# Four landing tiles for weights in a pool of their own, in layer 0 and layer 1's first half

## The chip, the core and the metric

The kernel runs on one core of one Trainium2 chip. The core's engines are TensorE (PE: matmuls, with a weight load, PEld, beside each), VectorE (DVE), ScalarE (ACT), GpSimd (POOL) and SyncE (SP), which issues all of this kernel's DMAs. The metric is the device time of one execution in microseconds.

## The reference

One inference step of a decoder trunk with two layers and width D = 1024, for a prompt of 1024 tokens and for 8 short sequences of 4 tokens (32 sample tokens), each with states of its own. Cut to what matters here:

```
def trunk(x):                       # rows of 1024 prompt tokens, or of 32 sample tokens
    h = x
    # layer 0 (even): S5 and HGRN2 side by side
    u, z_a, q, f, i, z_b = split(rmsnorm(h, norm_w[0]) @ even_w_in)     # 1024 x 3072
    y = gelu(s5(u))                                                     # complex diagonal state space
    a = y * sigmoid(y @ ssm_glu_w + glu_b) * silu(z_a)                  # 512 columns
    b = rms(hgrn2(silu(q), sigmoid(-f), i)) * silu(z_b)                 # 4 heads, 512 columns
    h = h + concat(a, b) @ even_w_out                                   # 1024 x 1024
    # layer 1 (odd): RWKV-7
    xn = rmsnorm(h, norm_w[1]);  xx = previous_row(xn) - xn
    xr, xw, xk, xv, xa, xg = (xn + xx * mix[m] for m in range(6))
    r, k, v, z = xr @ W[0], xk @ W[1], xv @ W[2], xg @ W[3]             # rw_w_rkvz, 1024 x 1024 each
    decay = exp(-c * sigmoid(w0 + tanh(xw @ w1) @ w2));  a = sigmoid(a0 + (xa @ a1) @ a2)
    g = sigmoid(xg @ g1) @ g2
    y, state = rwkv7_scan(r, decay, k, v, kk, a, state)                 # 16 heads of 64
    h = h + ((groupnorm(y) + bonus) * g * silu(z)) @ rw_w_o
    return rmsnorm(h, final_norm_w), all states
```

## The kernel before

Activations lie with the width on the partitions and the tokens along the free axis, in two halves: the first 512 tokens, and the other 512 with the 32 sample tokens (544 columns, as two cuts of 272). All matmuls are done in parts: each operand is split into a rounded high part and the rest, and each product of a weight tile (128x128) and an operand is the sum of three, high by high, high by low, low by high (`dense2`, line 805: `wh`,`xh`; `wh`,`xl`; `wl`,`xh`).

A weight is a column block of 128 out of a matrix, with eight tiles of 128 rows. `weights2` makes it: two DMAs of 256 KB each bring four row tiles into a **landing tile** `ws` (line 784); ACT copies it into the high part `wh` (line 70), DVE subtracts that from `ws` and writes the low part `wl` (line 72). `wh` and `wl` have two buffers each, so the next weight's are written when the matmuls with the last but one are done. The landing tile, too, has two buffers, in the pool `wp` with `wh` and `wl`. A landing tile comes free when `wl` has been made from it. `lora_weights` does the same for the low-rank weights `w1` and `a1` of RWKV-7, but for each half of the rows it takes two landing tiles: `ws`, which is loaded, and `wm`, into which POOL multiplies the same weights by `mix` (line 961).

The operands come as pairs, `xh` and `xl`, from `pair`: nine pairs in the pool `xx`, and in one stage `nxe` more, in the pool `xe` that exists only there (the second loop over `first` in `halves`: layer 1's first half, after the output projection of layer 0 has ended).

The program runs in stages. **Layer 0**: the input projection (`proj_in`) of half 1 and half 0 for the first four column blocks, then the other twenty blocks of each half, woven with S5 and the HGRN2 heads; `l1_vectors` loads small vectors of layer 1 (`mix`, by elements of 4 bytes) after the second block and makes `omix` from it on DVE (line 885). **Output of layer 0** (`glu`, `proj_out`): the S5 branch's gate, four weights, then eight weights of `even_w_out`, first for half 0 and then for half 1, this woven with the first steps of layer 1 (`l1_first`, which begins with `lora_weights`). Operands of the S5 branch and the heads are split by `cut` or `cut_in` (`gh`, `gl`). **Layer 1, first half**: k, r, v and the gate's first weights; then `layer1` runs the recurrence (chains over `ZR` and `BK`, which go through DRAM, line 1514) woven with the second half's projections, and the output projection.

The program's text gives the order only in part. A tile scheduler plays it through with estimated times and writes out for each engine one order, which the engine then follows; on SP this is the order of the DMA issues. Making a weight has high priority in it, so a DMA of a weight is put where a landing tile is estimated to be free. So another number of tiles changes the order on every engine.

Of the kernel before, what the change touches and what calls it, by code (L numbers as in the profile page):

```python
# [9 lines left out]
F32 = mybir.dt.float32  # L10
# [26 lines left out]
class Builder:  # L37
    def __init__(self, tc, I, O):
        self.tc, self.nc, self.I, self.O = tc, tc.nc, I, O
        self.load = {"act": 0.0, "dve": 0.0}  # L40
        self.tsz, self.inv = (200, 200, 160), [("v", 0, 32)]
        self.evb, self.ahead = 1.5, 4
        self.wcount, self.wpool, self.ev8 = 0, 0, [None, None]
        self.wp8 = dict(k=0, r=0, v=0), dict(k=1, r=1, v=1)
        self.pairs, self.nxe, self.per, self.xe = 0, 5, 2, None
        self.ly, self.lt = 4, (2, 4)
        self.lead = 2
        self.rate0, self.rate, self.rate2 = (1.4, 2.2, 1.0, 0.75), 1.5, 2.0
        self.nxh = 9
# [726 lines left out]
    def weights2(self, src, nk, m=128, name="w"):  # L776


        with self.tc.high_priority():
            wh = self.wp.tile([128, nk, m], F32R, tag="wh", name=f"{name}h", bufs=2)  # L780
            wl = self.wp.tile([128, nk, m], F32R, tag="wl", name=f"{name}l", bufs=2)
            for k in range(0, nk, 4):
                ke = min(k + 4, nk)
                ws = self.wp.tile([128, 4, m], F32, tag="ws", name=f"{name}s", bufs=2)
                if isinstance(src, list):
                    for h in range(2):
                        self.dma(ws[64 * h:64 * h + 64], src[k // 4].rearrange("p (k m) -> p k m", m=m))
                else:
                    self.dma(ws[:, :ke - k], src.rearrange("(k p) m -> p k m", p=128)[:, k:ke])
                self.wcount += 1  # L790
                self.split(wh[:, k:ke], wl[:, k:ke], ws[:, :ke - k], lo_pool=self.wcount % 8 < self.wpool)
        return wh, wl
# [157 lines left out]
    def lora_weights(self, names):  # L950

        with self.tc.high_priority():
            T = lambda tag: self.wp.tile([128, KT, 128], F32R, tag=tag, name=tag, bufs=2)
            plain, scaled = (T("wh"), T("wl")), (T("wh"), T("wl"))
            for k in range(0, KT, 4):
                ws, wm = (self.wp.tile([128, 4, 128], F32, tag="ws", name="ws", bufs=2) for i in range(2))
                for i, (nm, m) in enumerate(names):
                    cs = slice(64 * i, 64 * i + 64)
                    self.dma(ws[:, :, cs], self.I[f"rw_{nm}1"][0].rearrange("(k p) m -> p k m", p=128)[:, k:k + 4])
                    j = m * KT + k  # L960
                    self.nc.gpsimd.tensor_tensor(out=wm[:, :, cs], in0=ws[:, :, cs], op=ALU.mult,
                                                 in1=self.mix[:, j:j + 4].unsqueeze(2).broadcast_to([128, 4, 64]))
                for (h, l), x in ((plain, ws), (scaled, wm)):
                    self.split(h[:, k:k + 4], l[:, k:k + 4], x)
        return plain, scaled
# [860 lines left out]
    def build(self):  # L1826
        tc, nc, I = self.tc, self.nc, self.I
        dt = lambda name, shape: tc.dram_tile(shape, F32, name=name)
        self.xT_d = [dt(f"xT{k}", [128, NT]) for k in range(KT)]
        self.pr_d = {m: dt(f"pr{m}", [128, NT]) for m in range(4, 24)}  # L1830
        self.u_d = [dt(f"u{m}", [128, 8, 144]) for m in range(4)]
        self.y_d = [dt(f"y{m}", [128, 8, 136]) for m in range(4)]
        self.cat_d = [dt(f"cat{m}", [128, NT]) for m in range(4)]
        self.h1_d = [dt(f"h1{m}", [128, NT]) for m in range(KT)]

        H = lambda nm, sh: [[dt(f"{nm}{h}{g}", sh) for g in range(2)] for h in range(2)]
        self.zr_d, self.bk_d = H("zr", [128, 8, NP, 2, 64]), H("bk", [128, 8, NP, 2, 64])
        self.vc_d = H("vc", [128, 8, NP, 64])
        self.n_d, self.x_d, self.xn_d = H("nd", [128, 8, NP, 32]), H("xd", [128, 8, NP, 64]), H("xnd", [32, 2, 8, NP, 32])

        self.g1_d, self.g2_d = ([dt(f"{x}{h}", [128, 8, KT, 64]) for h in range(2)] for x in ("g1", "g2"))
        self.g1s_d, self.g2s_d, self.os_d = (dt(x, [128, KT, 32]) for x in ("g1s", "g2s", "os"))
        self.o_d = [dt(f"o{h}", [128, KT, 512]) for h in range(2)]
        self.pc_d = [dt(f"pc{m}", [2, NB, 64]) for m in range(KT)]
        for nm in ("r", "k", "v", "sw", "a"):
            setattr(self, f"{nm}_d", [dt(f"{nm}d{m}", [128, NT]) for m in range(KT)])
        self.rk_d = [dt(f"rkd{m}", [128, NT]) for m in range(KT)]
        with tc.tile_pool(name="cst", bufs=1) as self.cp:
            self.constants()
            self.nw0 = self.vec(I["norm_w"][0], "nw0")  # L1850
            with ExitStack() as st:
                self.pools(st)
                with ExitStack() as aux:
                    self.layer0(aux)
                with ExitStack() as aux:
                    self.halves(aux)

    def run(self, *gs, back=None):

# [68 lines left out]

            self.run((rest(), 1), (hgrn, self.rate0[2]))

    def halves(self, st):

        P = lambda name, st, **kw: st.enter_context(self.tc.tile_pool(name=name, bufs=1, reuse_waits="tile", **kw))
        R = lambda name, st: P(name, st, side="right")
        with ExitStack() as right:
            self.dp0, self.diff = R("diff", right), []
            with ExitStack() as r:
                op = R("out", r)
                with ExitStack() as t:
                    gp = P("glu1", t)  # L1940
                    glu = self.glu(1, gp, op)
                    next(glu)
                    self.heads_out(1, op)
                    next(glu)
                    self.norm1(0, lambda: gp.tile([128, 544], F32, tag="n", name="n", bufs=3))
                    for _ in glu:
                        pass
                rk = P("rwk", st)
                self.l1_pools(st)
                self.rwkv_constants(rk)  # L1950
                self.l1_constants(rk)
                self.made = {"v": [0, 0], "g": [0, 0], "x": 0, "o": [0, 0, 0], "first": False}
                self.ah, first = None, self.l1_first(0)
                self.run((self.proj_out(1), 1), back=(first, self.rate0[3]))
            self.ah, self.xe = R("ahead", right), R("xe", right)
            for _ in first:
                pass
            self.xe, gate = None, self.l1_gate(0)
            next(gate)
        self.ch = R("chn", st)  # L1960
        self.layer1(gate)

# [46 lines left out]
```

## Time and profile before

| what | us |
|---|---|
| median of 3 runs | 1949.92 |
| lowest and highest run | 1946.46, 1953.49 |
| profiled execution | 1946.68 |
| its span | 1945.0 |
| PE busy | 1736.1 (89%) |
| DVE busy | 1256.1 (65%) |
| ACT busy | 979.8 (50%) |
| POOL busy | 507.5 (26%) |

The mean granted clock of PE in the profiled execution is 0.903 of its full speed. The DMA queues moved 308.40 MB. The profile's views used below are the timeline of an engine (start, duration, instruction, and in brackets the idle time before it with what ended it), the waits of an engine summed by what it waited for, a tile's view (what its handlers waited for, and who waited for them), and windows (busy time of each engine in a stretch, granted clock, mean share of busy DMA engines, GB/s). A DMA share near 1 means that all 16 DMA engines are at work throughout.

### The profile page before, as it was taken

Reading aid. Unit: us, or ns where it says so; the run is one execution under the profiler, and the core shown is the slowest. Engines: PE = TensorE matmul, PEld = TensorE weight load, DVE = VectorE, ACT = ScalarE, POOL = GpSimd, SP = SyncE. Lnnn points to the kernel's source line nnn. Section 1 sums busy time; section 2 is a strip of 40 time slices with the busy share of each in tenths; the row PEclk is TensorE's granted clock in tenths of the full one; section 3 lists DMA queues with packets and bytes.
Section 4 is the critical chain, followed back from the end, with each engine's and each line's share of the span. In section 5 each row is a group of like instructions: output and inputs, shape, how many; then the busy total and the mean of one; then the engine's idle time right before and its main releaser. Section 6 shows DMA issues by size and latency. Waiting matters only on the chain. (4 is left out here: it accounts for less than half of the span.)

```text
span 1945.0 us, 39798 instructions
## 1 busy us (share of the span) xinstructions
PE 1736.1 (89%) x15060; PEld 1437.8 (74%) x15060; DVE 1256.1 (65%) x2700; ACT 979.8 (50%) x1887; POOL 507.5 (26%) x567
## 2 busy tenths in 40 slices
PE   6989889889979689998579999999899999999977
PEld 5767768788868577576447787888788888778776
DVE  5887778655554953689585852478979454655543
ACT  6345656354553434753345756565547434534464
POOL 2413535323221500001042410133322112331231
PEclk9989989887889899898779997999799899998799
DMA  9545444433544446699928424469795666544453
GB/s 242 150 128 153 112 116 134 121 112 107 154 148 152 128 150 199 199 243 263 247 66 219 140 88 129 130 168 276 191 235 160 164 160 166 151 130 128 121 151 112
DMA packets 555013, 308.40 MB, mean 159 GB/s; under 512 B 284884, under 2 KB 489044, under 8 KB 554821
## 3 DMA queue, kind: packets, MB, share of 16 engines
q1 hardware_dynamic: 554820, 305.86, 57.3%
q8 instruction: 119, 1.95, 0.4%
q14 instruction: 74, 0.60, 0.1%
HBM read 199.76 MB, written 104.81 MB: 157 GB/s over the span
## 5 line engine op out<-in xcount | busy, mean ns | idle before, releaser
L805 PE MATMUL dps<-xh,wh 128*128 128x272 f32 (+3 forms) x1696 | 589.5, 353 | 59.4 <-ACT wh L70 25.0
L805 PE MATMUL dps<-xl,wh 128*128 128x272 f32 (+3 forms) x1696 | 585.3, 347 | 7.8 <-DVE xl L72 6.1
L805 PE MATMUL dps<-xh,wl 128*128 128x272 f32 (+3 forms) x1696 | 581.9, 345 | 5.1 <-DVE wl L72 4.9
L805 PEld LDWEIGHTS dps<-xh,wh 128*128 128x128 f32 x1696 | 335.2, 200 | 110.6 <-ACT wh L70 29.9
L805 PEld LDWEIGHTS dps<-xh,wl 128*128 128x128 f32 x1696 | 338.6, 200 | 48.6 <-DVE wl L72 11.2
L805 PEld LDWEIGHTS dps<-xl,wh 128*128 128x128 f32 x1696 | 338.6, 200 | 47.7 <-DVE xl L72 8.2
L70 ACT ACTIVATE wh<-ws 128x512 fp32r<-128x512 f32 (+1 forms) x336 | 198.8, 620 | 331.8 <-PE dps L805 181.7
L72 DVE TENSOR_TENSOR wl<-ws,wh 128x512 fp32r<-128x512 f32 (+1 forms) x321 | 238.2, 756 | 139.3 <-ACT wh L70 125.5
L1514 PE MATMUL m<-ZR,BK 64*128 64x128 f32 x512 | 68.3, 311 | 10.4 <-DMA ZR<-zr 10.4
L1514 PEld LDWEIGHTS m<-ZR,BK 64*128 64x128 f32 x512 | 56.9, 206 | 19.6 <-DMA ZR<-zr 10.5
L70 ACT ACTIVATE xh<-mm 128x256 fp32r<-128x256 f32 (+1 forms) x112 | 52.9, 483 | 34.0 <-DVE mm L944 15.0
L805 PE MATMUL dps<-gh,wh 128*128 128x272 f32 (+1 forms) x176 | 56.3, 321 | 11.3 <-ACT wh L70 4.3
L72 POOL TENSOR_TENSOR xl<-mm,xh 128x256 fp32r<-128x256 f32 (+1 forms) x40 | 33.1, 828 | 111.6 <-ACT xh L70 89.0
L805 PE MATMUL dps<-gh,wl 128*128 128x272 f32 (+1 forms) x176 | 55.4, 316 | 7.3 <-DVE wl L72 7.3
L805 PE MATMUL dps<-gl,wh 128*128 128x272 f32 (+1 forms) x176 | 55.8, 317 | 5.6 <-DVE gl L72 5.6
L1411 DVE TENSOR_TENSOR sT<-sX,sN 128x31 f32<-128x31 f32 (+15 forms) x124 | 50.3, 405 | 5.2 <-DMA sN<-nd 2.8
L1417 DVE TENSOR_TENSOR sX<-sX,sT 128x31 f32<-128x31 f32 (+15 forms) x124 | 50.8, 410 | 2.3
L72 POOL TENSOR_TENSOR e<-ek,e 128x512 fp32r<-128x512 f32 (+1 forms) x16 | 22.0, 1376 | 114.5 <-ACT e L70 87.9
L72 DVE TENSOR_TENSOR xl<-mm,xh 128x512 fp32r<-128x512 f32 (+2 forms) x72 | 42.6, 599 | 12.7 <-PE t L1104 7.3
L64 ACT ACTIVATE ev<-dps 128x272 f32<-128x272 f32 (+1 forms) x65 | 29.4, 452 | 41.9 <-PE dps L805 36.4
L66 DVE COPY ev<-dps 128x272 f32<-128x272 f32 (+1 forms) x43 | 22.4, 523 | 42.9 <-PE dps L805 36.3
L805 PEld LDWEIGHTS dps<-gh,wh 128*128 128x128 f32 x176 | 36.0, 205 | 16.3 <-ACT ev L723 4.8
(651 smaller groups left out, 3676.4 us busy)
## 6 DMA issues: line engine op xcount, KB each, us to landing
ws<-in_rw_w_rkvz SPq DMA_DIRECT2D x128, 256.0 KB
ws<-in_even_w_in SPq DMA_DIRECT2D x96, 256.0 KB
ws<-in_rw_w_o SPq DMA_DIRECT2D x48, 256.0 KB
ws<-in_even_w_out SPq DMA_DIRECT2D x32, 256.0 KB
BK<-bk SPq DMA_DIRECT2D x32, 256.0 KB
ZR<-zr SPq DMA_DIRECT2D x32, 256.0 KB
pr<-ev SPq DMA_DIRECT2D x20, 272.0 KB
pr<-ev SPq DMA_DIRECT2D x20, 256.0 KB
```

Source lines behind the costliest of these rows:

```text
L64: return self.nc.scalar.activation(out, in_, AF.Copy)
L66: return self.nc.vector.tensor_copy(out, in_)
L70: self.nc.scalar.activation(hi, x, AF.Copy)
L72: e.tensor_tensor(out=lo, in0=x, in1=hi.bitcast(F32), op=ALU.subtract)
L805: mm = lambda c0, n, i, u, k, v: self.nc.tensor.matmul(ps[c0], u[:, k, :], v[:, c0:c0 + n], start=i == 0, stop=i == len(terms) - 1)
L1411: E.tensor_tensor(out=w, in0=X[:, s0:s0 + m, j:j + 1].broadcast_to([128, m, n]), in1=N[:, j, j + 1:32].unsqueeze(1).broadcast_to([128, m, ...
L1417: E.tensor_tensor(out=X[:, s0:s0 + m, j + 1:32], in0=X[:, s0:s0 + m, j + 1:32], in1=w, op=ALU.subtract)
L1514: nc.tensor.matmul(f2(pm[h][:, q]), f2(BK[hr, q]), f2(ZR[hr, q]), start=True, stop=True)
```

## The change

The landing tiles get a pool of their own, `ws`, on the right side of SBUF, with four buffers. It is opened ahead of layer 0 and closed after the gate's first weight in layer 1's first half; from there on a pool `ws1` with two buffers takes its place, as before. The number of additional operand pairs, `nxe`, goes from 5 to 4, so 13 pairs instead of 14 in the stage of layer 1's first half.

```diff
--- before.py
+++ after.py
@@ -42,7 +42,7 @@
         self.evb, self.ahead = 1.5, 4
         self.wcount, self.wpool, self.ev8 = 0, 0, [None, None]
         self.wp8 = dict(k=0, r=0, v=0), dict(k=1, r=1, v=1)
-        self.pairs, self.nxe, self.per, self.xe = 0, 5, 2, None
+        self.pairs, self.nxe, self.per, self.xe = 0, 4, 2, None
         self.ly, self.lt = 4, (2, 4)
         self.lead = 2
         self.rate0, self.rate, self.rate2 = (1.4, 2.2, 1.0, 0.75), 1.5, 2.0
@@ -781,7 +781,7 @@
             wl = self.wp.tile([128, nk, m], F32R, tag="wl", name=f"{name}l", bufs=2)
             for k in range(0, nk, 4):
                 ke = min(k + 4, nk)
-                ws = self.wp.tile([128, 4, m], F32, tag="ws", name=f"{name}s", bufs=2)
+                ws = self.ws.tile([128, 4, m], F32, tag="ws", name=f"{name}s", bufs=self.nws)
                 if isinstance(src, list):
                     for h in range(2):
                         self.dma(ws[64 * h:64 * h + 64], src[k // 4].rearrange("p (k m) -> p k m", m=m))
@@ -953,7 +953,7 @@
             T = lambda tag: self.wp.tile([128, KT, 128], F32R, tag=tag, name=tag, bufs=2)
             plain, scaled = (T("wh"), T("wl")), (T("wh"), T("wl"))
             for k in range(0, KT, 4):
-                ws, wm = (self.wp.tile([128, 4, 128], F32, tag="ws", name="ws", bufs=2) for i in range(2))
+                ws, wm = (self.ws.tile([128, 4, 128], F32, tag="ws", name="ws", bufs=self.nws) for i in range(2))
                 for i, (nm, m) in enumerate(names):
                     cs = slice(64 * i, 64 * i + 64)
                     self.dma(ws[:, :, cs], self.I[f"rw_{nm}1"][0].rearrange("(k p) m -> p k m", p=128)[:, k:k + 4])
@@ -1850,10 +1850,12 @@
             self.nw0 = self.vec(I["norm_w"][0], "nw0")
             with ExitStack() as st:
                 self.pools(st)
+                early = st.enter_context(ExitStack())
+                self.ws, self.nws = early.enter_context(tc.tile_pool(name="ws", bufs=1, reuse_waits="tile", side="right")), 4
                 with ExitStack() as aux:
                     self.layer0(aux)
                 with ExitStack() as aux:
-                    self.halves(aux)
+                    self.halves(aux, early)
 
     def run(self, *gs, back=None):
 
@@ -1928,7 +1930,7 @@
 
             self.run((rest(), 1), (hgrn, self.rate0[2]))
 
-    def halves(self, st):
+    def halves(self, st, early):
 
         P = lambda name, st, **kw: st.enter_context(self.tc.tile_pool(name=name, bufs=1, reuse_waits="tile", **kw))
         R = lambda name, st: P(name, st, side="right")
@@ -1957,6 +1959,8 @@
                 pass
             self.xe, gate = None, self.l1_gate(0)
             next(gate)
+        early.close()
+        self.ws, self.nws = R("ws1", st), 2
         self.ch = R("chn", st)
         self.layer1(gate)
```

The scheduler's order moves with it. **SP, start of the program**, before: `ws` are transfers of 256 KB, `xt` are the token rows that the first projection needs, `mix` is the gather.

```order
L52 DMA ws<-in_even_w_in 128x4x128 x2
L52 DMA nw_208<-in_norm_w 128x8x1
L52 DMA xt<-in_x_sample 32x1024
L52 DMA xt<-in_x_prompt 128x1024 x3
L52 DMA ws<-in_even_w_in 128x4x128
L52 DMA xt<-in_x_prompt 128x1024
L52 DMA ws<-in_even_w_in 128x4x128
L52 DMA nw_715<-in_norm_w 128x8x1
L52 DMA mix<-in_rw_mix 128x48x1
```

The same place after the change:

```order
L52 DMA ws<-in_even_w_in 128x4x128 x4
L52 DMA nw_208<-in_norm_w 128x8x1
L52 DMA xt<-in_x_sample 32x1024
L52 DMA xt<-in_x_prompt 128x1024
L52 DMA ws<-in_even_w_in 128x4x128
L52 DMA xt<-in_x_prompt 128x1024
L52 DMA ws<-in_even_w_in 128x4x128 x2
L52 DMA xt<-in_x_prompt 128x1024
L52 DMA ws<-in_even_w_in 128x4x128
L52 DMA xt<-in_x_prompt 128x1024
L52 DMA nw_718<-in_norm_w 128x8x1
L52 DMA mix<-in_rw_mix 128x48x1
```

Three transfers of weights stood ahead of the fourth `xt` of the prompt and four ahead of `mix`; now eight stand ahead of both.

**ACT, start of the output projection of layer 0's first half**, before: `wh_5949` is its first weight (in two halves, from `ws_5951` and `ws_5955`), `wh_5988` the second; `gh` are casts of the S5 output `y` of the other half.

```order
L723 ACTIVATE ev_5900<-dps_5901,glub_725 128x512
L70 ACTIVATE gh_6299<-y_6282 128x544
L70 ACTIVATE wh_5949<-ws_5951 128x512
L723 ACTIVATE ev_5929<-dps_5930,glub_725 128x512
L70 ACTIVATE gh_6303<-y_6287 128x544
L70 ACTIVATE wh_5949<-ws_5955 128x512
L70 ACTIVATE xh_5916<-ev_5900 128x512
L70 ACTIVATE xh_5945<-ev_5929 128x512
L70 ACTIVATE gh_6313<-o_6311 128x544
L70 ACTIVATE gh_6307<-y_6292 128x544
L70 ACTIVATE wh_5988<-ws_5990 128x512
L70 ACTIVATE wh_5988<-ws_5994 128x512
```

The same place after the change (`wh_5952` is the first weight, `wh_5991` the second, `gh_6302` and `gh_6306` answer to `gh_6299` and `gh_6303`):

```order
L70 ACTIVATE xh_5861<-ev_5845 128x512
L70 ACTIVATE xh_5890<-ev_5874 128x512
L70 ACTIVATE wh_5952<-ws_5954 128x512
L70 ACTIVATE wh_5952<-ws_5958 128x512
L723 ACTIVATE ev_5903<-dps_5904,glub_728 128x512
L70 ACTIVATE gh_6302<-y_6285 128x544
L70 ACTIVATE wh_5991<-ws_5993 128x512
L723 ACTIVATE ev_5932<-dps_5933,glub_728 128x512
L70 ACTIVATE gh_6306<-y_6290 128x544
L70 ACTIVATE wh_5991<-ws_5997 128x512
```

Both halves of the first weight now stand ahead of both casts of `y`; of the second weight, one half does.

**SP, the low-rank weights of layer 1**, before, from the last constants to the next weights of layer 0's output projection; the loads of the low-rank weights' second half stand ten rows ahead of these:

```order
L52 DMA w2s<-in_rw_g 128x128
L52 DMA w2s<-in_rw_g 32x128
L52 DMA xd_121<-sX 128x1024 x2
L52 DMA xd_122<-sX 128x1024 x2
L52 DMA xd_123<-sX 128x1024
L52 DMA w2s<-in_rw_g 128x128
L52 DMA ws<-in_even_w_out 128x4x128
L52 DMA w2s<-in_rw_g 32x128
L52 DMA xd_123<-sX 128x1024
L52 DMA xd_124<-sX 128x1024 x2
L52 DMA h_97<-res 128x544
L52 DMA ws<-in_even_w_out 128x4x128
```

The same place after the change, from the low-rank weights' first half on:

```order
L52 DMA ws<-in_rw_w 128x4x64
L52 DMA ws<-in_rw_a 128x4x64
L52 DMA za<-pr_67 128x544
L52 DMA za<-pr_68 128x544
L52 DMA ws<-in_rw_w 128x4x64
L52 DMA ws<-in_rw_a 128x4x64
L52 DMA res<-xT_57 128x544
L52 DMA ws<-in_even_w_out 128x4x128 x2
L52 DMA w2s<-in_rw_g 128x128
L52 DMA w2s<-in_rw_g 32x128
L52 DMA k_k<-in_rw_k_k 128x8x1
```

The two transfers of `even_w_out` stood behind the constants and among the zero states `xd`; now they come right behind the second low-rank half and one residual load, ahead of the constants.

## Rows read from the trace of the kernel before

**Rows 1.** The page: the span; busy us and share of each engine

```profile
span 1945.0 us, 39798 instructions
...
PE 1736.1 (89%) x15060; PEld 1437.8 (74%) x15060; DVE 1256.1 (65%) x2700; ACT 979.8 (50%) x1887; POOL 507.5 (26%) x567
```

**Rows 2.** PE's waits, 0 to 970 us: us in total, times, longest

```profile
PE dps L805 <- ACT wh L70: 25.2, 8, 7.2
PE dps L805 <- DVE wl L72: 10.9, 5, 6.1
```

**Rows 3.** SP's waits, 0 to 960 us

```profile
SPq L52 <- DVE wl L72: 138.3, 80, 13.5
```

**Rows 4.** Tile `ws`, 0 to 960: idle before it until...; who waited for it

```profile
  PE dps L805: 134.9, 37
...
  PE dps L805: 36.0, 13
```

**Rows 5.** Timeline, start: start us, us, instruction, idle before and releaser

```profile
17.98 0.19 DVE L885 TENSOR_SCALAR omix<-mix 128x48 f32<-128x48 f32 x1 [3.15 <-DMA mix<-in_rw_mix]
...
24.83 0.52 PE L805 MATMUL dps<-xh,wh 128*128 128x272 f32 x2 [1.33 <-ACT xh L70]
```

**Rows 6.** Windows, start: us, busy of five engines, PEclk, DMA share, GB/s

```profile
4.00:6.00 2.00, 0.00 (x0) 0.00 (x0) 0.78 (x2) 1.07 (x2) 0.00 (x0) 1.00 1.10 173
6.00:12.00 6.00, 3.02 (x16) 2.36 (x16) 1.73 (x8) 5.90 (x18) 0.00 (x0) 1.00 1.03 382
```

**Rows 7.** Timeline at the first output weight: PE, ACT, DVE

```profile
580.48 0.80 PE L805 MATMUL dps<-xh,wh 128*128 128x512 f32 x1 [6.58 <-ACT wh L70]
...
579.25 0.66 ACT L70 ACTIVATE gh<-y 128x544 fp32r<-128x544 f32 x1 [3.81 <-DVE y L713]
...
577.50 1.68 DVE L711 COPY y<-yl 128x512 f32<-128x512 f32 x1
```

**Rows 8.** Windows around it

```profile
574.00:580.40 6.40, 0.00 (x0) 0.00 (x0) 5.44 (x6) 2.59 (x5) 4.70 (x3) 0.68 0.51 145
580.40:584.00 3.60, 3.31 (x7) 2.20 (x8) 3.60 (x8) 2.14 (x5) 0.00 (x0) 0.50 0.20 58
584.00:590.00 6.00, 6.00 (x22) 4.78 (x22) 5.09 (x9) 3.44 (x7) 0.00 (x0) 0.79 0.81 235
590.00:596.00 6.00, 6.00 (x28) 4.89 (x27) 3.15 (x6) 3.01 (x6) 0.00 (x0) 1.00 0.42 132
```

**Rows 9.** Timeline at the low-rank weights: POOL, PE, SP

```profile
650.75 11.11 POOL L961 TENSOR_TENSOR ws<-ws,mix 128x256 f32<-128x256 f32 x2 [3.68 <-DVE wl L72]
...
650.73 0.60 PE L805 MATMUL dps<-gh,wl 128*128 128x272 f32 x1 [6.13 <-DVE wl L72]
...
674.43 1.21 SPq L52 DMA_DIRECT2D ws<-in_even_w_out  x1
...
679.50 1.15 SPq L52 DMA_DIRECT2D ws<-in_even_w_out  x1
...
686.41 0.60 PE L805 MATMUL dps<-gh,wh 128*128 128x272 f32 x1 [4.30 <-ACT wh L70]
...
688.87 0.59 PE L805 MATMUL dps<-gh,wl 128*128 128x272 f32 x1 [1.18 <-DVE wl L72]
```

**Rows 10.** Windows behind them

```profile
686.40:690.00 3.60, 2.41 (x9) 2.09 (x10) 3.54 (x7) 1.78 (x3) 0.00 (x0) 0.50 0.03 8
690.00:696.00 6.00, 6.00 (x41) 6.00 (x40) 5.42 (x10) 2.54 (x5) 0.00 (x0) 0.80 0.43 129
```

**Rows 11.** Timeline, layer 1's first half: PE

```profile
949.02 0.80 PE L805 MATMUL dps<-xh,wh 128*128 128x512 f32 x1 [7.16 <-ACT wh L70]
...
971.61 1.64 PE L1514 MATMUL m<-ZR,BK 64*128 64x128 f32 x7 [10.37 <-DMA ZR<-zr]
```

**Rows 12.** Windows of it

```profile
780.00:860.00 80.00, 76.06 (x458) 52.42 (x459) 57.87 (x89) 46.91 (x75) 1.94 (x4) 0.89 0.75 210
860.00:972.00 112.00, 82.36 (x660) 60.51 (x659) 87.23 (x184) 45.52 (x79) 15.15 (x24) 0.83 1.03 256
```


## The prediction

> **What bounds the kernel now.** I read the page first: TensorE (PE) is busy for 1736.1 of the 1945.0 us of the span, so some 209 us are idle on the engine that sets the end, and DVE, the next, for 1256.1 [rows 1]. A change that computes nothing less can win only out of the idle 209 us, and out of the matmuls that run at a lower granted clock after a stall. Next come PE's waits in the stretch in which the change has force, 0 to 970 us: for the high half of a weight (`wh`, cast by ScalarE, ACT) it waits 25.2 us in 8 waits, for the low half (`wl`, subtracted by VectorE, DVE) 10.9 us in 5, together 36.1 us [rows 2]. Then the question whether the landing tile is what is late. SyncE (SP), which issues every DMA in one order, stands 138.3 us in the same stretch, 80 times, until a `wl` has been made, which is when a landing tile comes free [rows 3]. That looks like the bound and is mostly none: in the view of the landing tile, the engines that handle it sat idle for 134.9 us until a matmul of PE was over, so the weights were there and the operand buffers `wh`/`wl` (two each, untouched) were not free. Only 36.0 us are PE's own waits behind the tile [rows 4]. The prize is at most these 36 us and the slowed matmuls behind them; what has to be asked of each is whether the landing tile made it late, or an engine that does its work in order.
>
> **Start, 0 to 45 us: a cost.** Two more landing tiles let the order put more weights ahead of the prompt's rows `xt`: eight transfers of 256 KB now stand ahead of the fourth `xt`, where three did. None is wanted early; the first projection waits for `xt`, and starts at 24.83 us [rows 5]. The DMA engines are full from the beginning (share 1.10 and 1.03), at 173 GB/s while weights land and 382 GB/s while mostly `xt` does [rows 6]. A transfer of 262 kB takes 1.5 us at the one rate and 0.7 at the other; I take 1.25, nearer to the first, where weights land, so five more are 6.2 us. Not all of this counts, since the fourth `xt` is not waited for alone: DVE stood until 17.98 us for `mix` [rows 5], a gather that is issued right behind these transfers and shifts with them by at most that sum, and behind it the new order has a split of weights (0.69 us) less on DVE and one reciprocal chain already done. So +6.2 less some 2: I take **+4 us**, with bounds 0 (the weights fill gaps that the gather leaves) and +9 (five at 1.5 us, and the fourth `xt` behind a transfer that must first wait for its own tile, some 1.5 us). The Trainium skill, "DMA: Bandwidth & Descriptors", section "Rules for kernel authors", says to issue a DMA early, compute, and wait late, since then the fixed setup overlaps. By this rule the start would cost 0 and the sum below would be 4 us lower; the full DMA engines of these rows speak against it here, since an early transfer takes its time from one that is awaited.
>
> **First output weight of layer 0, 573 to 596 us: a gain.** PE waits 6.58 us at 580.48 for a `wh`. ACT had the landing tile's data, but stands in its order before a cast of `y` which waits 3.81 us for DVE (579.25); the weight's cast is the next. DVE itself works on until 579.2, last on a copy of that `y`, 1.68 us from 577.50 [rows 7]. With four tiles the second half's transfer no longer waits for the first weight's, and the cast is put ahead of both casts of `y` on ACT. Had that been all, 6.58 us would go, and what the slowed matmuls cost: after PE stood for these 6.58 us its granted clock is 0.50 of full speed (the 1.2 GHz level) for 3.6 us and 0.79 in the 6.0 us after, so 1.8 + 1.3 = 3.1 us [rows 8]. But the next late thing is close. In PE's new order 18 of the first weight's 24 terms stand ahead of the second weight, at 6.00 us for 28 matmuls, 0.21 each [rows 8], 3.9 us of work for the gap; then the second weight's second half is late, whose cast is still behind a `y`, and that copy still ends at 579.2. Of the 3.9 us some goes to the first weight's `wl`, which DVE, 5.44 of these 6.40 us busy [rows 8], has to make earlier. I take **-3 us**, with bounds 0 and -9.7.
>
> **Low-rank weights and the return to the output projection, 646 to 696 us: a gain.** Each half of the low-rank weights takes a loaded and a scaled tile, so before the change one half fills both. GpSimd (POOL) scales the first half from 650.75 to 661.86, and only then can the second half be loaded; the next output weights follow at 674.43 and 679.50, behind small constant loads and zero states `xd` [rows 9]. PE then waits 4.30 us for `wh` at 686.41 and 1.18 us for `wl` at 688.87; the clock after it is 0.50 for 3.6 us (2.41 us of them busy) and 0.80 for 6.0, worth 1.2 + 1.2 = 2.4 us [rows 10], so 7.9 us in all [rows 9]. In the new order the second low-rank half has tiles of its own and both output transfers stand ahead of the constants. The first tile comes free with POOL's first multiply, at 661.9, some 12 us before the old issue. Next late is ACT, whose new order casts these weights before the low-rank evictions, so little is left: I take **-6 us**, with bounds 0 (ACT or DVE arrive there late anyway) and -7.9. The 6.13 us that PE waits for a `wl` at 650.73 are no part of it [rows 9]: that is the subtraction's place in DVE's order, which moves by a few rows only.
>
> **Layer 1's first half, 860 to 972 us: almost nothing.** Here stands the largest single wait for a weight, 7.16 us at 949.02, and 10.37 us at 971.61 for `ZR` from DRAM [rows 11]. But the DMA engines are full from 860 to 972 (share 1.03), at 256 GB/s [rows 12]. Two more tiles hold 524 kB, which at 256 GB/s is 2.0 us of transfers done ahead; the bytes to be moved up to `ZR` are the same. So what PE doesn't wait for at 949 it waits for at 971: **-2 us**, with bounds +4 (`ZR` behind two more weights, 2.0 us, twice) and -8 (the wait at 949 goes and `ZR` isn't later).
>
> **One operand pair less**, 13 in place of 14 in the stage at 780 to 950 us. PE is busy for 76.06 of the first 80 us of it [rows 12], so it has little to lose before the DMA engines fill. Two changes of operand set lie in it; at each the new set starts one pair later, about 1.4 us of DVE work. That is hidden while PE has the other pairs' terms: +0.5 us, bounds 0 and +3. **The order of everything else**, reordered by the scheduler in 0 to 970 us, I put at 0, bounds -6 and +6; the size is that of its larger single waits [rows 7, 9]. The tile pool's move and `early.close()` compute nothing.
>
> **The sum**: +4 - 3 - 6 - 2 + 0.5 = -6.5 us. The profiled execution took 1946.68 us in all, its span 1945.0; it would become 1940.2. The median of the three runs is 1949.92, 3.2 us above the profiled one, and it is against that median that the time will stand: **1943.4 us**, -0.33%. The measurement can tell about 0.3%, 5.9 us, from no change, so the forecast sits just past that line.
>
> **Rivals.** (1) *All waits for landing go.* The rule behind it is in the Trainium skill, "Perfetto Trace Analysis", section "Optimization Strategy": the same gap repeating on the engine that should be saturated can mean that there isn't enough SBUF for the next tile. As a mechanism of this kernel: each of the 13 waits of 36.1 us [rows 2] goes, and with them the slowed matmuls of 580 and 686, 5.5 us, less the start's 4: -37.6 us, 1912. The 134.9 us of idleness until PE was done [rows 4] speak against it. With two thirds of it, as far as the tile and not an engine's order makes them late, 1925.
> (2) *Absorbed.* The waits at 580 and 686 only move on to DVE, which is busy at the first 5.44 of 6.40 us [rows 8], and the DMA stage gives back the rest: +4 - 1 - 2 + 0 = +1, that is 1951. To it belongs the case that the change doesn't do what it says: with `wh` and `wl` still in twos, the casts stay where they were and only DMAs are earlier: 1949 to 1951.
> (3) *Slower: weights crowd out what is awaited.* One mechanism, at the start: transfers of weights that nobody waits for stand in SP's one order ahead of `xt` and `mix`. At its upper bound it costs +9, with -1 from 580 and 686 each if DVE holds them: +7, and 1957. It decides from the point at which the first projection's matmul starts later than some 32 us, rather than 24.83. For it: the DMA share over 1 in both rows of the start [rows 6]. Against: the projection is short of DVE too, and may take up slack.
> (4) *Slower by order.* Fewer pairs and `ZR` behind weights in the full stage, +3 and +4, and the order elsewhere at +6 against the gains of 9: +8, 1958.
>
> **Chances.** The forecast's case, 1936 to 1948: 0.42, of which 0.31 lie past the line of 0.3%. Rival 1: 0.12. Rival 2: 0.17. Rival 3: 0.17. Rival 4: 0.12. Faster is then 0.31 + 0.12 = 0.43, same 0.11 + 0.17 = 0.28, slower 0.29. The range that leaves out two in ten cuts the far parts of rivals 1, 3 and 4: 1928 to 1959; the likeliest case's own is 1936 to 1948.
>
> **What would show it.** Start: the first `L805` matmul near 29 us instead of 24.83; at 25 or sooner, the term is wrong. At 580: PE's wait for `wh` split in two shorter ones. At 686: no wait over 2 us for `wh`, and the SP issue of that weight near 662 to 672. At 949 and 971: the sum of the two waits within some 3 us of 17.5 and the DMA share still over 1. If the waits for `wh` and `wl` up to 970 us fall from 36 to under 10 us and the time falls by 25, rival 1 was right; if they fall and the time doesn't, the waits went to names that I haven't priced, and the prediction is wrong in its reordering term.

## The result and the profile after

The changed kernel takes 1928.63 us (median of 4 runs, 1926.58 to 1932.37) against 1951.7 of the kernel before in the same comparison; the ratio is 0.9884, with a 95% interval of 0.9851 to 0.9916. So it is faster, by 16 to 29 us, where 6.5 were forecast. In later comparisons the kernel before had medians of 1946.77 to 1948.13 over 17 to 32 runs (single runs from 1935 to 1960), which leaves the gain at 18 to 20 us. One run of experiment 6 fell in a slower state and is left out of its median. The two executions with a trace differ by less, 1946.68 and 1932.37, spans 1945.0 and 1930.6: the traced execution of the changed kernel is its slowest. The sums below are of these two spans, -14.4 us.

From the page of the changed kernel, to be held against [rows 1]:

```profile
span 1930.6 us, 39826 instructions
...
PE 1717.5 (89%) x15060; PEld 1421.8 (74%) x15060; DVE 1263.1 (65%) x2700; ACT 983.4 (51%) x1890; POOL 516.6 (27%) x567
```

PE's busy time fell by 18.6 us with the same 15060 matmuls, and its idle time rose from 208.9 to 213.1 us. **All of the gain in this pair of traces is time in which matmuls ran, none is time in which PE waited.** PE's waits up to 970 us, to be held against [rows 2] (us in total, times, longest):

```profile
PE m L1514 <- DMA ZR<-zr: 20.2, 2, 11.0
...
PE dps L805 <- DVE gl L72: 10.7, 3, 6.6
...
PE m L1548 <- DMA DA<-xnd: 7.8, 1, 7.8
...
PE dps L805 <- DVE wl L72: 7.1, 4, 3.1
...
PE dps L805 <- ACT wh L70: 0.5, 2, 0.3
```

The waits for the high half of a weight went from 25.2 us to 0.5, those for the low half from 10.9 to 7.1: the change does what it says, and takes away 28.5 us of waiting for weights. Waits for `ZR` and `xnd` from DRAM (28.0 us here; before, one of 10.37 us for `ZR` at 971.61, just past these 970 us) and for `gl` (5.6 before, 10.7 now) took their place.

To see where the time went, both executions are cut at the same points of the program: the first projection matmul, the 450th and 1050th matmul of `dense2`, the first matmul of the S5 gate (`gh`), the last one of layer 0's output projection, and the matmuls of the norm of layer 1's second half. Worked out from these two timelines and the windows between: "low" is PE's busy time times what the granted clock lacks of 1, summed over windows of 2.5 us.

| stretch | before, us (PE idle, low) | after, us (PE idle, low) | difference |
|---|---|---|---|
| to the first projection matmul | 24.8 (13, 0) | 28.4 (17, 0) | +3.5 |
| to the 450th matmul | 124.4 (15, 10) | 116.6 (13, 3) | -7.7 |
| to the 1050th matmul | 220 (27, 14) | 221 (30, 10) | +0.4 |
| to the first gate matmul | 191.4 (15, 29) | 173.6 (9, 17) | -17.8 |
| output of layer 0 | 210.6 (34, 13) | 208.5 (30, 13) | -2.1 |
| layer 1, first half | 217.5 (42, 24) | 217.8 (47, 22) | +0.3 |
| the rest (two tiles in both) | 956.2 (62, 69) | 965.2 (66, 78) | +9.0 |

The row with most in it is the second half of the input projection with S5 and HGRN2. Before and after, as windows (us; busy us of PE, PEld, DVE, ACT, POOL with counts; granted clock; DMA share; GB/s):

```profile
369.30:560.70 191.40, 176.57 (x1124) 157.73 (x1123) 98.79 (x198) 92.17 (x143) 54.08 (x42) 0.84 0.40 119
```

```profile
365.50:539.10 173.60, 164.68 (x1115) 146.73 (x1113) 100.47 (x193) 94.57 (x144) 51.06 (x42) 0.90 0.45 131
```

About as many matmuls (1124 and 1115) kept PE busy for 176.57 us at a mean granted clock of 0.84, and for 164.68 us at 0.90. PE waits for no weight here in either, so this gain is no wait for weights that went. Some 12 of the 17.8 us are time in which matmuls ran, 6 are idle time of PE, which waits here for operands of S5 and the heads.

### The profile page after: what moved, and what is told of

It reads as the page before. It is cut to its first block, busy times and chain, and to the rows that moved or that the text cites. A ratio compares the mean times of both kernels' runs of the same rounds, so it can differ in the third digit from the quotient of the medians.

```text
span 1930.6 us, 39826 instructions
## 1 busy us (share of the span) xinstructions
PE 1717.5 (89%) x15060; PEld 1421.8 (74%) x15060; DVE 1263.1 (65%) x2700; ACT 983.4 (51%) x1890; POOL 516.6 (27%) x567
## 5 line engine op out<-in xcount | busy, mean ns | idle before, releaser
L805 PE MATMUL dps<-xh,wh 128*128 128x272 f32 (+3 forms) x1696 | 582.6, 349 | 42.4 <-ACT xh L70 18.5
L805 PE MATMUL dps<-xh,wl 128*128 128x272 f32 (+3 forms) x1696 | 572.6, 339 | 5.9 <-DVE wl L72 5.7
L805 PEld LDWEIGHTS dps<-xh,wh 128*128 128x128 f32 x1696 | 329.1, 196 | 95.6 <-ACT xh L70 22.1
L805 PEld LDWEIGHTS dps<-xl,wh 128*128 128x128 f32 x1696 | 332.6, 196 | 54.1 <-DVE xl L72 10.9
L805 PEld LDWEIGHTS dps<-xh,wl 128*128 128x128 f32 x1696 | 332.8, 197 | 41.4 <-DVE wl L72 9.6
L72 DVE TENSOR_TENSOR wl<-ws,wh 128x512 fp32r<-128x512 f32 (+1 forms) x321 | 243.9, 778 | 105.8 <-ACT wh L70 104.0
L1344 POOL COPY ZB<-e 128x8 f32<-128x8 f32 x16 | 8.7, 543 | 141.3 <-DVE e L1322 73.2
L1571 PE MATMUL m<-ZM,DT 64*64 64x128 f32 x512 | 42.5, 296 | 2.9 <-DVE MR L1517 2.9
```

What stands on the lines that cost most here:

```text
L72: e.tensor_tensor(out=lo, in0=x, in1=hi.bitcast(F32), op=ALU.subtract)
L805: mm = lambda c0, n, i, u, k, v: self.nc.tensor.matmul(ps[c0], u[:, k, :], v[:, c0:c0 + n], start=i == 0, stop=i == len(terms) - 1)
L1571: nc.tensor.matmul(pd[hr, q], DT[hr, q], ZM[hr, q], start=True, stop=True)
```

## The experiments

The theories set against each other are these. *Waits*: the gain is that of the waits for weights, above all at the output projection. *Order*: it stands in the input stage, whose new order has fewer stretches at the lower clock. *Luck*: those stretches fall differently in each execution of one order. Then, once it was seen that the gain stands in the input stage: *tiles*, four tiles make that stage quicker, against *draw*, any other order moves it by as much and four tiles drew a good one.

**1. The pool alone.** The changed kernel with two tiles and five pairs:

```diff
-self.pairs, self.nxe, self.per, self.xe = 0, 4, 2, None
+self.pairs, self.nxe, self.per, self.xe = 0, 5, 2, None
...
-...tc.tile_pool(name="ws", bufs=1, reuse_waits="tile", side="right")), 4
+...tc.tile_pool(name="ws", bufs=1, reuse_waits="tile", side="right")), 2
```

> The landing tiles in their own pool, but two of them, and five additional pairs as before. Every engine's order is that of the kernel before up to about 970 us. All theories: no change, ratio 0.998 to 1.002, first output matmul of layer 0's gate (gh) at 560.7 us within 2 us. Theory ORDER (the gain of the change stands in the input stage of layer 0, where PE's idle time is unchanged and its matmuls run less often at the lower granted clock, because another order of the same matmuls gives fewer such stretches): time lost to the lower clock from 365 us to the end of the input projection again about 26 us, as before (after the change 14). Theory LUCK (the clock's low stretches fall differently in each execution): some 14 to 26 us there, with the same order.

Measured: 1946.18 us, ratio 0.999 (0.9969 to 1.001). The first gate matmul is at 561.4 us, and the low-clock time from the 1050th matmul to it is 29 us, as before. The pool's place costs nothing, and in this stretch the same order gives the same low-clock time. (Experiment 3 shows that this does not hold everywhere.)

**2. One pair less alone.** The kernel before with `nxe` 4 (the first line of the diff the other way round).

> Two landing tiles as before, four additional pairs instead of five: that part of the change alone. The order is that of the kernel before up to about 860 us. My prediction's term: +0.5 us, bounds 0 to +3, so 1950 to 1953 and a ratio of 1.000 to 1.002. A rival: the stage after 860 us is full of DMA, and every shift of the order there moves the wait for ZR by several us either way: -6 to +6. Theory ORDER: low-clock time from 365 us to the end of the input projection about 26 us again; theory LUCK: 14 to 26.

Measured: 1970.88 us, ratio 1.0107 (1.0081 to 1.0134), so 20 us slower. None of it is where the pairs are: in its trace layer 1's first half takes 214.2 us, 3.3 less than before. The rest of the program, where the pairs no longer exist and the source is the same, takes 981 us against 956. An order that was changed in one stage goes on into the next.

**3. Four tiles in the input stage alone**, then two, and five pairs:

```diff
         self.run((dense(), 1), (s5s(), self.rate0[0]), back=(hgrn, self.rate0[1]))
+        self.early.close()
+        self.ws, self.nws = self.early.enter_context(tc.tile_pool(name="ws2", ..., side="right")), 2
```

> Four landing tiles through layer 0's input stage (projection, S5, HGRN2), then two, and five additional pairs. The order is that of the changed kernel up to about 520 us. Theory ORDER: the input stage keeps its gain, the first gate matmul (gh) at 539 us within 4 us, and the whole at 1929 to 1936, ratio 0.988 to 0.993. Theory WAITS (the gain is that of the waits for weights at 580 and 686 us): 1950 to 1954, the start's +3.5 us and nothing else. Theory LUCK: gh anywhere from 539 to 561 us.

Measured: 1928.94 us, ratio 0.9887 (0.9861 to 0.9913): the whole gain. The waits at the output projection are not the cause. The first gate matmul is at 546.5 us, 3.5 past what theory *order* allowed; with the same order the changed kernel had 539.1, so one order does vary, by 7 us here and by 4 in the four executions with the order of before (557.2, 559.5, 560.7, 561.4). Most of the 7 us is luck of the clock: up to 508 us every engine has the same order in these two traces, yet from the 450th matmul to the 1050th the low-clock time is 23 us here and 10 in the changed kernel, while PE's idle time is 25 against 30. The stretch from there to the gate repeats, 175.1 us against 173.6, as the 191 us of the order of before do, so the 17.8 us won in it go with the order. But luck is not small elsewhere, and a difference of some 7 us between two single traces shows nothing by itself.

**4. Four tiles from the output projection on**, two in the input stage, four pairs (the same two lines, with 2 first and 4 in the second).

> Two landing tiles through layer 0's input stage, then four up to the gate's first weight of layer 1, and four additional pairs. The order is that of the kernel before up to about 540 us. Theory ORDER: first gate matmul (gh) at 560.7 us within 3 us as before, then the predicted gains at 580 and 686 (-2.3 and -4.6 in the two traces so far) and nothing in the DMA-full stage: 1941 to 1946, ratio 0.995 to 0.998. Theory WAITS: 1928 to 1936. Theory LUCK: gh anywhere from 539 to 561.

Measured: 1950.81 us, ratio 1.0018 (0.9996 to 1.004): no gain. Output of layer 0: 206.7 us against 210.6 and layer 1's first half 215.8 against 217.5, which the rest, 960 against 956, gives back. The two later stages in which four tiles are in force are worth 5.6 us here, and 1.8 in the changed kernel. Theory *waits* falls; the 1941 to 1946 of theory *order* was missed too, since the gain of these stages didn't reach the total.

**5 and 6. Another order, with two tiles and with four.** The pace at which HGRN2 heads are woven into the projection is one of the numbers by which the program's text is ordered; a small change of it leaves the work and gives another order from about 200 us on:

```diff
-self.rate0, self.rate, self.rate2 = (1.4, 2.2, 1.0, 0.75), 1.5, 2.0
+self.rate0, self.rate, self.rate2 = (1.4, 2.1, 1.0, 0.75), 1.5, 2.0
```

> Two landing tiles and five additional pairs as before, but the pace at which HGRN2 heads are woven into the input projection is 2.1 in place of 2.2: another order of the same work from about 200 us on, with no landing tile more. Theory TILES (the input stage is quicker because weights land earlier): first gate matmul (gh) within 4 us of the kernel before's 557 to 561 us. Theory DRAW (any other order of the input stage moves it by 10 us and more, because it moves the stretches at the lower clock; the four tiles drew a good one): gh anywhere from 540 to 575, and low-clock time from the 1050th projection matmul to gh anywhere from 15 to 35 us, where the order of before gives 28 to 30.

> The kernel with four landing tiles in the input stage alone (then two, five pairs), with the same pace of 2.1. Theory TILES: gh at 539 to 547 us, as with the pace of 2.2, and 12 to 20 us ahead of the two-tile kernel with the pace of 2.1. Theory DRAW: gh anywhere from 535 to 570, on either side of the two-tile kernel's.

Measured: with two tiles 1961.71 us and the gate at 554.5, which both theories allowed; with four 1950.85 us and the gate at 557.2. At this pace the trace shows no gain of four tiles in the input stage, so theory *tiles* falls as a rule for every order. The same stretch as above, of the four-tile kernel at this pace:

```profile
368.40:557.20 188.80, 176.21 (x1114) 157.12 (x1112) 103.50 (x195) 93.01 (x142) 55.09 (x42) 0.84 0.40 118
```

The clock is 0.84 again and the busy time 176.21 us, as in the kernel before.

**7. Token rows first.** The changed kernel with

```diff
+            with self.tc.high_priority():
-            self.dma(t[:q], I["x_prompt"][...] if i < 4 else ...)
+                self.dma(t[:q], I["x_prompt"][...] if i < 4 else ...)
```

> The changed kernel, with the loads of the token rows xt at high priority, so that they stand ahead of all weights but one at the start. My term for the start (+4, seen as +3.5): the first projection matmul at 24 to 26 us instead of 28.4, and mix, now behind five weights rather than eight, lets it start earlier. If nothing else moved: 1925, ratio 0.986. The order changes from the start, so theory DRAW: gh anywhere from 532 to 565 and a total of 1915 to 1950; theory TILES: gh at 535 to 541.

Measured: 1950.36 us, ratio 1.0009 (0.9984 to 1.0035). The timeline of PE, its first projection matmul:

```profile
25.14 0.82 PE L806 MATMUL dps<-xh,wh 128*128 128x272 f32 x2 [1.31 <-ACT xh L70]
```

The start's cost is gone, 25.14 instead of 28.37 us, which shows that the weights ahead of `xt` and `mix` were its cause. All the rest of the input stage's gain is gone with it: the gate is at 569.0, the latest of all. The better start drew a worse order, by a little more than theory *draw* had allowed (565, and 1950 in all).

**8. Three tiles and five pairs.**

> Three landing tiles in place of four, and all five additional pairs (2 KB less for the tiles, which is what the fifth pair lacked). Theory TILES: half to all of the gain of the input stage, gh at 540 to 552, total 1930 to 1940. Theory DRAW: gh anywhere from 535 to 570, total 1920 to 1960. Term of the pair (+0.5): not to be told apart here.

Measured: 1960.59 us, ratio 1.0071 (1.0046 to 1.0097). The gate is at 542.5, the output of layer 0 takes 205.4 us, the shortest of all, and then layer 1's first half takes 223.0 and the rest 982: a quick input stage lost again later. The gate is where both theories had it; the total is past what either allowed.

**9 to 12. Two more orders, each with two and with four tiles** (paces of 1.45 and 1.35 for the S5 pieces, in place of 1.4).

> Two landing tiles, five additional pairs; the pace of the S5 pieces in the input stage 1.45 in place of 1.4, another order from about 200 us on. Theory DRAW: gh anywhere from 540 to 575, total 1930 to 1970. Theory TILES: gh 554 to 562, as in the five two-tile executions so far. In both: 90 to 92 us from the 150th to the 450th projection matmul, where the waits for weights are.

> Four landing tiles in the input stage alone, the same pace of 1.45. Theory TILES: gh 12 to 20 us ahead of the two-tile kernel of this pace. Theory DRAW with a small share that is the tiles' own (start +3.5 us, and 84 to 86 us instead of 90 to 92 from the 150th to the 450th projection matmul, so -2.5 in all): gh 2 us ahead in the mean, from 15 ahead to 15 behind; at the 450th matmul 1 to 4 us ahead.

> As two_pace_145 with a pace of 1.35. Theory DRAW: gh anywhere from 540 to 575. Theory TILES: 554 to 562.

> Four landing tiles in the input stage, the same pace of 1.35. Theory TILES: gh 12 to 20 us ahead of the two-tile kernel of this pace. Theory DRAW with the small share of the tiles' own: from 15 us ahead to 15 behind; at the 450th projection matmul 1 to 4 us ahead.

Measured, with all the others, cut as above (us; "to the gate" is the stretch from the 1050th matmul, with the mean clock of its window; tiles are those of the input stage; "output" has an asterisk where four tiles are in force there, two where three are; the stages are those of one trace each; the medians of "before" and "after" are of the first comparison, in those of the others the kernel before had 1946.8 to 1948.1):

| kernel | tiles | 450th matmul | to the gate, clock | gate | output | layer 1, first half | rest | median |
|---|---|---|---|---|---|---|---|---|
| before | 2 | 149.2 | 191.4, 0.84 | 560.7 | 210.6 | 217.5 | 956 | 1951.7 |
| own pool | 2 | 149.4 | 191.3, 0.84 | 561.4 | 213.2 | 216.4 | 951 | 1946.2 |
| pairs 4 | 2 | 148.9 | 188.6, 0.85 | 557.2 | 212.7 | 214.2 | 981 | 1970.9 |
| four in output | 2 | 148.4 | 191.5, 0.84 | 559.5 | 206.7* | 215.8 | 960 | 1950.8 |
| after | 4 | 145.0 | 173.6, 0.90 | 539.1 | 208.5* | 217.8 | 965 | 1928.6 |
| four in input | 4 | 146.4 | 175.1, 0.89 | 546.5 | 211.1 | 215.4 | 960 | 1928.9 |
| rows first | 4 | 156.5 | 184.9, 0.86 | 569.0 | 210.4* | 217.5 | 956 | 1950.4 |
| three tiles | 3 | 147.8 | 175.6, 0.90 | 542.5 | 205.4** | 223.0 | 982 | 1960.6 |
| pace 2.1 | 2 | 148.8 | 182.6, 0.88 | 554.5 | 212.3 | 216.8 | 976 | 1961.7 |
| pace 2.1 | 4 | 149.5 | 188.8, 0.84 | 557.2 | 213.2 | 215.8 | 965 | 1950.9 |
| pace 1.45 | 2 | 148.2 | 175.9, 0.87 | 551.8 | 213.6 | 216.7 | 967 | 1956.4 |
| pace 1.45 | 4 | 148.3 | 177.4, 0.87 | 552.5 | 210.6 | 217.3 | 987 | 1965.0 |
| pace 1.35 | 2 | 150.4 | 181.7, 0.87 | 554.6 | 211.2 | 220.7 | 988 | 1974.2 |
| pace 1.35 | 4 | 146.7 | 173.3, 0.89 | 542.8 | 208.8 | 223.8 | 987 | 1961.2 |

In the four pairs that differ in the input stage's tiles alone (own pool and four in input; the three paces) four tiles put the gate at -14.9, +2.7, +0.7 and -11.8 us, -5.8 in the mean. In the totals the pairs differ by -17.2, -10.9, +8.6 and -13.0.

At the 450th matmul the four differ by -3.0, +0.7, +0.1 and -3.7; the expectation of 1 to 4 us there held in two pairs of four. But these are not four orders: the paces change the order of no engine before some 184 us, so up to the 450th matmul seven kernels with two tiles share one order, and five with four tiles another. Read so, the 450th matmul comes at 148.2 to 150.4 us with two tiles and at 145.0 to 149.5 with four, 1.9 us earlier in the mean. From the 150th matmul to the 450th these kernels take 89.6 to 90.6 us with two tiles and 83.5 to 85.0 with four, about as was expected; most of it is lost ahead of the 150th, which comes at 58.6 to 60.1 us and at 61.4 to 64.5.

What stands is this. Four tiles do not make the input stage quicker under every order, and the order (with luck) decides over more than the tiles do: the gate lies between 539.1 and 569.0 us with four. But theory *draw* was too strong as well. It had any other order move the gate by 10 us and more; the three other orders with two tiles gave 551.8 to 554.6, less than 10 us ahead of the order of before (557.2 to 561.4), and none came near 539.1 or 542.8. What is the tiles' own is an estimate of some 6 of the 15 to 22 us that the input stage gained (the mean of the four pairs). With single traces that vary by 7 us under one order, it is not shown beyond doubt that this share isn't zero. No version beat the changed kernel; "four in input" equals it.

## Why the prediction was right, and where it was not

The direction and the range (1928 to 1959) held, the range by 0.6 us, but not for the reason given. The time lies below the forecast's own case (1936 to 1948) and above that of rival 1. The stages that the prediction priced came to +1.7 us together in the traces, where -6.5 were forecast; all of the gain, and more, stands in the term that it put at 0. That the direction was right is luck. By the steps:

- **Start, +4.** Right, and by the cause given: +3.5. The timeline of DVE and PE, to be held against [rows 5], shows the gather `mix` later by 3.8 us and the projection with it:

```profile
21.81 0.19 DVE L885 TENSOR_SCALAR omix<-mix 128x48 f32<-128x48 f32 x1 [2.80 <-DMA mix<-in_rw_mix]
...
28.37 0.82 PE L805 MATMUL dps<-xh,wh 128*128 128x272 f32 x2 [0.49 <-ACT xh L70]
```

- **First output weight, -3.** Right in what is late next, too large in size: the 6.58 us of [rows 7] are gone, and waits of 2.07 and 1.71 us stand there instead. Counted from the first gate matmul, the changed kernel is 3.7 us ahead at the 1780th matmul of `dense2`, just behind that wait, and 0.5 us ahead at the 1950th, past both weights. That DVE is the next late thing can be read off the second wait:

```profile
547.27 0.50 PE L805 MATMUL dps<-gh,wh 128*128 128x512 f32 x1 [2.07 <-ACT ev L723]
...
556.80 0.50 PE L805 MATMUL dps<-xh,wl 128*128 128x512 f32 x1 [1.71 <-DVE wl L72]
```

- **Low-rank weights, -6.** Half right. No wait for `wh` is left, and SP issues the output weights at 632.14 us, 19 us earlier than before if the some 23 us won by then are allowed for ([rows 9]: 674.43). From the 2150th matmul of `dense2` to the 2200th, where those waits stood, the changed kernel is 8.1 us quicker; 7.9 were priced. But just ahead, from the 2100th to the 2150th, it is 5.7 us slower: PE waits for `gl`, 6.57 and 3.20 us instead of 2.70 and 2.95, since on DVE the split that makes it stands behind splits of layer 1's operands. With both terms the output of layer 0 was to win 9 us; it won 2.1 here, and over all kernels takes 206.7 to 210.4 us with four tiles there and 208.8 to 213.6 with two. The step that failed is "little is left": that DVE arrives late was named only as a bound, and it is what happened.

```profile
639.38 0.60 PE L805 MATMUL dps<-gl,wh 128*128 128x272 f32 x1 [6.57 <-DVE gl L72]
...
644.78 0.60 PE L805 MATMUL dps<-gl,wh 128*128 128x272 f32 x1 [3.20 <-DVE gl L72]
...
632.14 0.37 SPq L52 DMA_DIRECT2D ws<-in_even_w_out  x1
...
631.99 1.89 DVE L72 TENSOR_TENSOR xl<-h,xh 128x512 fp32r<-128x512 f32 x3
...
638.60 0.72 DVE L72 TENSOR_TENSOR gl<-ev,gh 128x544 fp32r<-128x544 f32 x1
```

- **Layer 1's first half, -2.** Right in its mechanism: waits for weights of 14 us in 860 to 972 went, and PE waits for `ZR` and `xnd` instead, 28.0 us where one wait of 10.4 stood in [rows 11]; the DMA engines are full as in [rows 12], and the stage as a whole came out at +0.3:

```profile
919.83 1.57 PE L1514 MATMUL m<-ZR,BK 64*128 64x128 f32 x6 [9.18 <-DMA ZR<-zr]
...
935.24 0.80 PE L1548 MATMUL m<-DA,MZ 32*32 32x32 f32 x16 [7.80 <-DMA DA<-xnd]
...
948.39 0.98 PE L1514 MATMUL m<-ZR,BK 64*128 64x128 f32 x3 [11.03 <-DMA ZR<-zr]
```

```profile
835.00:948.00 113.00, 81.08 (x674) 61.78 (x672) 86.93 (x184) 45.75 (x79) 16.36 (x25) 0.82 1.02 254
```

- **One pair less, +0.5.** Not borne out: in experiment 2 its stage is 3.3 us shorter, outside the bounds of 0 and +3, and the whole kernel is 20 us slower, since the rest, with another order, takes 25 us more.
- **The order of everything else, 0 with bounds of 6 either way.** Wrong, and this is where the whole gain stands. The stages with a priced term measured +3.5 (start), -2.1 (output of layer 0) and +0.3 (layer 1's first half), +1.7 in all, against +4, -9 and -1.5. No term was priced for the rest of the -14.4 us: -7.7 to the 450th matmul (PE idle 15.5 us before and 13.3 after, low clock 9.5 and 3.1), +0.4, -17.8 up to the gate, and +9.0 behind layer 1's first half, -16.1 together. This is the new order, with the share that the four tiles have of their own in the input stage, and with luck of the clock, which one pair of traces doesn't tell apart ahead of the 1050th matmul and behind layer 1's first half. I took the bound from single waits; what an order moves is above all the sum of many stretches at the lower clock, 157 us of PE's time in the trace before and 141 after. The prediction looked for slowed matmuls only behind a stall. The row to price it from was there: window by window the clock of that half of the projection stands at 0.5 nine times without a long wait ahead of most of them.

Of the rivals, the first (all waits for landing go: 1912 to 1925) names a time near the measured one and is not what happened: the waits went, and PE's idle time grew. Its sign on record, waits for `wh` and `wl` under 10 us and 25 us less in all, nearly came (7.6 us; 18 to 23 less by the medians), and would have misled: experiments 3 and 4 tell it apart. The sentence of the Trainium skill behind it ("Perfetto Trace Analysis", section "Optimization Strategy") agrees with the trace as to the gaps: with more buffers PE's waits for `wh` fell from 25.2 to 0.5 us. The time isn't told by them. The second (absorbed) is what became of the waits. For the start, the prediction read the rule on early DMAs in the Trainium skill ("DMA: Bandwidth & Descriptors", section "Rules for kernel authors") as a cost of nothing. The page speaks of the fixed setup alone; the traces show 3.5 us, and experiment 7 gives them back.

## What to carry to other kernels

Where a scheduler writes the order, a change of buffers is two changes: the one that is meant, and a new order of all that follows, here from 5 us less to 32 more in the rest of the program, where every version has the same source and two landing tiles. Separate them by giving the same edit to several orders (a pace, a number that is neutral in itself) and comparing pairs, and measure each stage between points of the program, not at the end; take more than one trace of each, since one order varied by 7 us here. A gain in TensorE's busy time with the same matmuls was for the most part a gain in granted clock here (15.7 of 18.6 us); look for it in the clock of windows. It isn't always so: from "own pool" to "four in input", whose traces differ by 9.5 us, idle time fell by 8.6 and the low-clock time rose by 4.7.

## What the runs showed of the hardware

Which work lowers the clock was not expected. In the second half of the input projection of the kernel before nine stretches at the lower clock cost 30.2 us together; four of them, and three or four in every other kernel, follow the piece of an HGRN2 head that treats the sample tokens, though PE is not idle in it. The timeline of that piece before, and windows around it:

```profile
382.13 0.40 PE L672 MATMUL xh<-atts,hvt 32*128 32x32 f32 x2
...
382.46 1.95 PE L675 MATMUL xh<-hq,hS 128*128 128x4 f32 x16
...
384.34 1.29 PE L683 MATMUL xh<-hvm,hkt 32*128 32x512 f32 x2
```

```profile
378.00:382.00 4.00, 4.00 (x35) 4.00 (x34) 2.99 (x7) 0.40 (x1) 2.91 (x2) 1.00 0.51 141
382.00:386.00 4.00, 4.00 (x24) 2.90 (x24) 1.89 (x3) 0.85 (x2) 1.80 (x2) 0.90 0.26 53
386.00:390.00 4.00, 4.00 (x12) 2.26 (x11) 2.50 (x5) 3.31 (x5) 0.78 (x2) 0.50 0.25 89
390.00:394.00 4.00, 4.00 (x16) 3.77 (x17) 0.64 (x1) 0.56 (x2) 0.00 (x0) 0.50 0.97 293
394.00:398.00 4.00, 4.00 (x27) 3.84 (x26) 0.00 (x0) 2.23 (x3) 0.00 (x0) 0.82 0.22 61
```

PE is busy for 4.00 of 4 us in each, sixteen matmuls have 4 columns and two have 32 rows, and the granted clock falls from 1.00 to 0.50 (the 1.2 GHz level) and comes back some 10 us later. Blocks of 32 matmuls with 32 columns (line 640) do it at some times and not at others. Windows with such a block, before (from 364.8 us) and after (from 355.3):

```profile
365.00:369.00 4.00, 4.00 (x34) 3.46 (x33) 1.16 (x3) 0.14 (x1) 0.00 (x0) 0.89 0.66 184
369.00:373.00 4.00, 4.00 (x25) 4.00 (x24) 2.07 (x7) 2.00 (x4) 0.00 (x0) 0.69 0.15 37
```

```profile
355.00:359.00 4.00, 4.00 (x37) 3.37 (x35) 2.74 (x3) 1.98 (x5) 2.52 (x3) 1.00 0.45 108
359.00:363.00 4.00, 4.00 (x34) 3.96 (x34) 2.77 (x10) 1.62 (x3) 1.06 (x1) 1.00 0.50 121
```

The block takes 4.0 us in the one and 3.8 in the other, right behind dense matmuls in both; the mean clock of the second window is 0.69 in the one and 1.00 in the other. The order alone does not decide it. "Four in input" has the order of the changed kernel here, and the same block, from 358.3 us, behind the same matmuls; there the clock falls:

```profile
358.00:362.00 4.00, 4.00 (x34) 3.38 (x33) 2.77 (x3) 2.01 (x5) 2.50 (x3) 0.90 0.45 111
362.00:366.00 4.00, 4.00 (x19) 3.87 (x19) 2.77 (x10) 1.20 (x2) 1.06 (x1) 0.50 0.43 101
```

Each such stretch costs 1.6 to 1.7 or 3.3 to 3.4 us, now and then 5 or 6.8 where another narrow piece lies in its wake. Nine of them before and six after (16.9 us) make 13.3 us of difference, and PE's idle time 6 us, together somewhat more than the 17.8 us of the stretch. What decides in each case whether such a block lowers the clock was not settled, and that the narrow matmuls are the cause is read from what stands ahead of each stretch; no kernel without them was run.
